# Two pairs of k-tiles of w_down: from direct column jobs behind the last run to the middle group of seven-product pairs

## The chip, the cores and the metric

The kernel runs on one core of a Trainium2 chip. The metric is the device time of one execution in microseconds (us); the figure given is the median of several runs. TensorE does the matmuls, VectorE (DVE), ScalarE (ACT) and GpSimd (POOL) the elementwise work, and the queues of SyncE (SP), ScalarE and POOL issue DMAs to 16 shared DMA engines.

## The reference

One encoder layer over 512 tokens of width 2048: a mixture of dilated window attention and gated linear attention, then a SwiGLU block, then a final RMSNorm. What matters here is the last step of the block and what follows it:

```python
h = rmsnorm(x, ffn_norm_w[l])
x = x + (jax.nn.silu(h @ w_gate[l]) * (h @ w_up[l])) @ w_down[l]   # (512 x 5632) @ (5632 x 2048)
return rmsnorm(x, final_norm_w)
```

All is float32. The kernel splits every operand of a large matmul into a high part (rounded to fp32r) and a low part (the rest), and sums three products: high by high, high by low, low by high.

## The kernel before, in words

The order of the instructions on every engine is written out by hand. TensorE, VectorE and ScalarE each work through their own instructions in program order; tiles come from pools of numbered slots, and a tile in a reused slot waits for the last users of the tile before it.

**Slots.** `s2` has 62 slots of 512 columns, `s4` 20 slots of 1024 columns, `ps` (in this phase "pu" in the profile) 8 PSUM banks. A slot is put back in program order and handed out oldest first (in `s4` a slot of the same kind first). One `s2` slot is held from the block's norm to the end (`rb[2]`).

**The product with w_down.** Its 5632 rows are 44 k-tiles of 128, taken as 22 pairs; its 2048 columns are four column blocks `c` of 512. The intermediate activations lie in DRAM (`gd`, one entry a pair). Before, the pairs are done in four ways, in this order:

- pairs 0 and 1: four direct column jobs (`job("B", ...)` with `evac_down`), 48 matmuls of 512 columns each, whose results are accumulated into `xd` in DRAM;
- pairs 2 to 17: class `Down`, seven-product pairs. A pair by a column block is a 2 x 2 block product with seven block products instead of eight. `Down.products` issues for each of the seven two token halves of three matmuls, 42 matmuls of 256 columns (lines 1625 to 1627);
- pairs 18 and 19: four more direct column jobs behind the runs (`evac_later`, `before_later`), lines 303 to 305, 48 matmuls of 512 columns each, whose results go straight to the residual;
- pairs 20 and 21 (`LAST = 40`): the tail (`finish`). It goes by token tiles `t` of 128, four column blocks each, 12 matmuls of 512 columns a block (lines 1815 to 1817); each block is added to the residual (`residual`, line 1449), squared on ScalarE (`squares`, line 409), and when a token tile is done its final norm is applied and it is sent out, so that only the last tile's end is uncovered.

**The runs of `Down`.** The pairs are in three groups X (2 to 7), Y (8 to 12) and Z (13 to 17), and there are ten runs, each a column block over some pairs:

```python
self.runs = [(0, X), (1, X), (2, X), (3, X + Y), (2, Y), (1, Y), (0, Y + Z), (1, Z), (2, Z), (3, Z)]
self.drop = {q: r for r, part in ((3, X), (6, Y), (9, Z)) for q in part}
```

A run holds seven banks. Runs 0 to 5 end with `evac`: each bank is copied to an `s2` slot and sent (or accumulated) to `md` in DRAM. A run from 6 on is `summed`: its seven partial results are fetched from `md` into seven `s2` slots (`fetch`, five pairs before the end of the run before) and copied into banks (`preload`, line 1598) while the last pair of the run before is multiplied; at its end `combine` (lines 1658 to 1675) makes the output of the column block, in seven steps that each put back a bank, and the generator `residuals` (line 1689), which is left on `urgent`, adds it to the residual tiles `x1[c]`.

**What a step needs.** The weights of a pair and column block are loaded by SP (line 1141), three sums are made on VectorE (`sums`, lines 1157 to 1159), and raw and sums are split: ScalarE casts the high part (line 1169), VectorE subtracts (line 1174). Where `by_dma` says so, the raw part's low part is made by an accumulating DMA of POOL instead (`part`, lines 1515 to 1517), and VectorE subtracts for the sums alone (line 1528).

**The activations' operands.** The generator `operands` makes a pair's: it loads `gd`, makes four differences (lines 1556 to 1559), and splits four sources (lines 1568 to 1572). It yields three times a pair; `make(n)` resumes it n times. A pair's operands hold 7 `s2` slots, from their making to the run named in `drop`. A pair is begun only if `len(s2.free) >= 9 + self.reserve`; the reserve is 4, and 11 in runs 4 and 5. If the pair of the step is not there yet, the loop makes it with no reserve. `make` is called behind the step's sums and splits and ahead of its matmuls.

**The stream of direct weights.** `st` loads the pieces of the direct jobs and of the tail (line 186; 512 KB each, two k-tiles) as long as fewer than `limit` are held, and `st.split(upto)` splits them half by half (line 201 on ScalarE, line 202 on VectorE). The direct jobs split three halves ahead, the later jobs a growing number ahead, so that all 16 halves of the tail are split under the later jobs. `g_load(j)` and `g_split(j)` load and split the activations of pair `j` for direct use (lines 1418, 1426 to 1430).

Of the kernel before, what the change touches and what calls it, by code (L numbers as in the profile page):

```python
# [120 lines left out]
def layer(nc, tc, x, attn_norm_w, w_in, rel_table, gw_f, gb_f, gw_b, gb_b, gla_norm_w, w_out,  # L121
# [7 lines left out]
    with tc.manual_schedule(), \  # L129
# [6 lines left out]
        s2 = Slots(p2, N2, 512, "a")  # L136
# [136 lines left out]
        def run_job(j):  # L273
# [6 lines left out]
            for i in range(j.n):  # L280
                if j.before:
                    j.before(i)
                st.load()
                st.split(j.first + i + AHEAD + (4 * j.tail + i if hasattr(j, "tail") else 0))
                _, _, wh, wl = st.halves[j.first + i]
# [1195 lines left out]
        class Down(Blocks):  # L1481
# [3 lines left out]
            def __init__(self, X, Y, Z):  # L1485
                self.runs = [(0, X), (1, X), (2, X), (3, X + Y), (2, Y), (1, Y), (0, Y + Z), (1, Z), (2, Z), (3, Z)]
                self.pairs = X + Y + Z
                self.drop = {q: r for r, part in ((3, X), (6, Y), (9, Z)) for q in part}
                self.begin([(r, q) for r, (c, part) in enumerate(self.runs) for q in part], 1, 256)
                self.x, self.parts, self.m, self.pre, self.seen = {}, {}, {}, [], set()  # L1490
                self.reserve = self.most = 4
                self.making = self.operands()

# [7 lines left out]
            def by_dma(self, i):  # L1501
                if i >= self.n:
                    return False
                r, q = self.seq[i]
                n = self.runs[r][1].index(q)
                return r == 3 or r == 6 and n > 5 or r > 6 and n in (0, 1, 4)

# [25 lines left out]
            def operands(self):  # L1533
# [14 lines left out]
                while raws or qs:  # L1548
                    load()
                    if not raws or len(s2.free) < 9 + self.reserve:  # L1550
                        yield
                        continue
# [142 lines left out]
            def run(self):  # L1695
                for i, (r, q) in enumerate(self.seq):
# [6 lines left out]
                    if left != 0:  # L1703
# [9 lines left out]
                        elif r != 3 and not self.by_dma(i + 2) and len(s4.free) > 4:  # L1713
                            self.sums(i + 3)
                            self.split(i + 2)
                    self.reserve = 11 if r in (4, 5) else 4
                    while q not in self.x:
                        self.reserve = 0
                        self.make(1)
                    self.make((r in (3, 6)) + i % 2)  # L1720
                    if n == max(len(part) - 5, 0) and r + 1 < len(self.runs) and self.summed(r + 1):
# [10 lines left out]
                    if r == len(self.runs) - 1:  # L1732
                        if n == 0:
                            g_load(LAST // 2 - 2)
                        if n == 2:
                            g_split(LAST // 2 - 2)
                            g_load(LAST // 2 - 1)
                            st.until, st.limit = None, 2
                            st.load()
                        if n == 3:  # L1740
                            st.split(later_first + 3)
                st.limit, st.big = 3, tail_first

        def evac_later(c):
            def f(banks):
                for t in range(4):
                    residual(c, t, banks[t])
            return f

        def before_later(c):  # L1750
            def f(i):
                j = LAST // 2 - 2 + (c + 1)
                if c and i == 0:
                    g_load(j)
                if i == (2 if c else 0) and c < 3:
                    g_split(j)
                run_urgent()
            return f

# [9 lines left out]
        down_pieces = len(st.pieces)  # L1769
        n_down = len(jobs)  # L1770
        later_first = len(st.halves)
        for c in range(4):
            j = job("B", [piece512(w_down, c * 512, k) for k in (LAST - 4, LAST - 2)], list(range(LAST - 4, LAST)),
                    lambda k: gT[k], evac_later(c), before=before_later(c), rate=1.0)
            j.tail = c
            if c == 3:
                j.drop = drop_g
        tail_first = len(st.halves)
        dn = Down(list(range(2, 8)), list(range(8, 13)), list(range(13, 18)))

# [10 lines left out]
        def finish():  # L1791

            first = len(st.halves)
            for c in range(4):
                st.add([piece512(w_down, c * 512, k) for k in range(LAST, 44, 2)])
            per = 44 - LAST

            def later(t, ys):
# [9 lines left out]
            def products(t, c, b, cols):  # L1808
                tok = slice(t * P, (t + 1) * P)
                o = b.t[:, cols]  # L1810
                for k in range(per):
                    st.split(first + c * per + k + 1)
                    _, _, wh, wl = st.halves[first + c * per + k]
# [57 lines left out]
        for n, j in enumerate(jobs):  # L1871
            if n == n_down:
                dn.run()
                start_tail()
            run_job(j)
            if n == n_out:
# [10 lines left out]
                ps = Slots(pcm.__enter__(), 8, 512, "pu")  # L1887
        drain()
        run_last()
# [28 lines left out]
```

## Time and profile before

| | us |
|---|---|
| median of three runs (lowest, highest) | 2190.3 (2189.37, 2192.0) |
| the profiled execution | 2190.92 |
| its span, first to last instruction | 2189.1 |

| phase of w_down in the profiled execution | start, us |
|---|---|
| direct jobs of pairs 0 and 1 | 1724.4 |
| runs 0 to 9 of `Down` | 1767.9 |
| direct jobs of pairs 18 and 19 | 2093.1 |
| tail | 2136.7 |
| last matmul starts | 2180.2 |

How to read it: the page gives for each engine its busy time and share of the span; a group of instructions by line has its count, busy time, mean duration and the idle time ahead of it with what ended that. In a list by order of time a row is start, length, engine, line, operation, output and inputs, count, and in square brackets the idle time of the engine ahead of it with its releaser. PE is TensorE's matmul and PEld its weight load. The listed duration of a matmul is longer than the distance between two of them, since they overlap; prices are taken from distances.

### The profile page before, as it was taken

The page shows a single profiled execution, that of the slowest core. Times are in us where ns is not written, and L with a number is a line of the kernel's source. Part 1 is how long each engine was busy: PE and PEld are TensorE (multiplying, and loading weights), DVE is VectorE, ACT ScalarE, POOL GpSimd, SP SyncE. Part 2 cuts the span into 40 slices and gives each one's busy share as a digit, 9 for nine tenths or more (in the row PEclk, how much of TensorE's full clock was granted, in tenths as well). Part 3 has the DMA queues.
Part 4 walks back from the last instruction along what each step waited for, and adds up shares of the span by engine and source line. Part 5 has one row for each costly group of instructions (what it writes and reads, how often), then busy time and mean ns, then how long its engine had stood idle before and what let it go on. Part 6 is the DMA issues. An engine that isn't in the chain of part 4 may idle for free.

```text
span 2189.1 us, 33329 instructions
## 1 busy us (share of the span) xinstructions
PE 2175.3 (99%) x12450; PEld 1908.5 (87%) x12450; DVE 1576.8 (72%) x2741; ACT 1217.8 (56%) x2032; POOL 325.4 (15%) x359
## 2 busy tenths in 40 slices
PE   9999999999999999999999999999999999999998
PEld 7888888888888888888888888888888899999987
DVE  4366665756456546888888888888888896888885
ACT  5344444444456436666666666666666665656642
POOL 0000000000000011222222222222222211121200
PEclk9999999999999999999999999999999999999999
DMA  6525635232222633889889898898888975888862
GB/s 210 161 84 142 162 90 144 91 97 87 97 87 88 211 106 103 195 193 210 203 195 211 192 211 202 196 211 193 208 204 198 288 183 172 240 212 230 254 220 77
DMA packets 255890, 375.19 MB, mean 171 GB/s; under 512 B 17999, under 2 KB 179455, under 8 KB 255728
## 3 DMA queue, kind: packets, MB, share of 16 engines
q1 hardware_dynamic: 188768, 252.03, 36.5%
q0 software_dynamic: 65776, 119.98, 28.1%
q8 instruction: 98, 1.61, 0.3%
q10 hardware_dynamic: 1184, 1.06, 0.2%
q14 instruction: 64, 0.52, 0.1%
HBM read 246.58 MB, written 35.19 MB: 129 GB/s over the span
## 4 chain that ended last, share of the span: by engine, by line
PE 94%; DVE 3%; DMA 2%; ACT 1%; issue 1%; SPq 0%; DVEq 0%; ACTq 0%
PE pd L1302 22%; PE pd L1308 11%; PE ps L303 5%; PE ps L304 5%; PE ps L305 5%; PE ps L295 5%; PE ps L296 5%; PE ps L297 5%; PE pe L1302 4%; PE pu L1626 4%; PE pu L1627 4%; PE pu L1625 4%; PE pe L1308 2%; DMA b<-in_w_down_dram 1%; PE pu L304 1%; PE pu L305 1%
## 5 line engine op out<-in xcount | busy, mean ns | idle before, releaser
L1302 PE MATMUL pd<-a,b 128*128 128x512 f32 x2112 | 528.4, 392 | 0.8 <-DVE a L1063 0.8
L1302 PEld LDWEIGHTS pd<-a,b 128*128 128x128 f32 x2112 | 378.9, 188 | 67.0 <-DVE a L1063 1.2
L1308 PEld LDWEIGHTS pd<-a,b 128*128 128x128 f32 x2112 | 288.5, 190 | 21.5
L1308 PE MATMUL pd<-a,b 128*128 128x256 f32 x2112 | 294.9, 282 | 0.0
L202 DVE TENSOR_TENSOR a<-b,a 128x512 fp32r<-128x512 f32 x288 | 193.1, 686 | 136.0 <-ACT a L201 124.1
L1209 POOL DMA_DIRECT2D b<-b x176 | 209.7, 1248 | 521.0 <-ACT b L1208 394.0
L1247 ACT CAST b<-b 128x1024 fp32r<-128x1024 f32 x176 | 185.3, 1053 | 166.3 <-DVE b L1233 138.4
L1626 PE MATMUL pu<-b,a 128*128 128x256 f32 x896 | 253.9, 283 | 0.9 <-DVE b L1174 0.9
L1625 PE MATMUL pu<-b,a 128*128 128x256 f32 x896 | 253.7, 283 | 0.5 <-ACT pu L1598 0.5
L1627 PE MATMUL pu<-b,a 128*128 128x256 f32 x896 | 253.5, 283 | 0.0
L1248 DVE TENSOR_TENSOR b<-b,b 128x1024 fp32r<-128x1024 f32 x176 | 214.9, 1221 | 50.3 <-ACT b L1247 26.4
L201 ACT CAST a<-b 128x512 fp32r<-128x512 f32 x288 | 170.2, 617 | 50.3 <-PE ps L305 22.3
L1626 PEld LDWEIGHTS pu<-b,a 128*128 128x128 f32 x896 | 172.0, 192 | 1.4 <-DVE b L1174 1.3
L1625 PEld LDWEIGHTS pu<-b,a 128*128 128x128 f32 x896 | 172.0, 192 | 0.9 <-ACT pu L1598 0.9
L1627 PEld LDWEIGHTS pu<-b,a 128*128 128x128 f32 x896 | 172.0, 192 | 0.0
L1330 DVE TENSOR_TENSOR a<-pd,a 128x512 f32<-128x512 f32 x132 | 91.4, 692 | 95.7 <-ACT a L1329 95.7
L1208 ACT ACTIVATE b<-b 128x768 fp32r<-128x768 f32 x176 | 149.1, 847 | 4.7 <-PE ps L305 2.9
L1210 ACT CAST b<-b 128x768 fp32r<-128x768 f32 x176 | 145.2, 825 | 0.6 <-PE ps L305 0.6
L1329 ACT COPY a<-pd 128x512 f32<-128x512 f32 x132 | 77.5, 587 | 102.0 <-PE pd L1308 102.0
L1230 DVE TENSOR_TENSOR b<-b 128x512 f32<-128x512 f32 x176 | 120.4, 684 | 0.0
L595 ACT CAST b<-ps 128x512 fp32r<-128x512 f32 x64 | 37.6, 587 | 142.9 <-PE ps L529 142.9
L295 PE MATMUL ps<-a,a 128*128 128x512 f32 x288 | 115.3, 400 | 0.0
(278 smaller groups left out, 4506.4 us busy)
## 6 DMA issues: line engine op xcount, KB each, us to landing
b<-b POOLq DMA_DIRECT2D x200, 384.0 KB, 5.5
b<-in_w_gate_dram SPq DMA_DIRECT2D x88, 512.0 KB, 3.8
b<-in_w_up_dram SPq DMA_DIRECT2D x88, 512.0 KB, 4.4
b<-in_w_down_dram SPq DMA_DIRECT2D x88, 512.0 KB, 6.3
b<-in_w_in_dram SPq DMA_DIRECT2D x48, 512.0 KB, 4.5
b<-in_w_in_dram SPq DMA_DIRECT2D x94, 256.0 KB, 4.2
b<-in_w_out_dram SPq DMA_DIRECT2D x32, 512.0 KB, 5.3
a<-a SPq DMA_DIRECT2D x96, 128.0 KB, 2.4
```

The source lines that it names most:

```text
L201: act.copy(h[2].t, r)
L202: dve.tensor_tensor(h[3].t, r, h[2].f, op=OP.subtract)
L295: mm(o, wh.t[:, c], xh.t, start=first, stop=False)
L1208: act.activation(lo.t, r, AF.Copy, scale=-1.0)
L1209: pool.dma_start(out=lo.f, in_=r, accum_op=OP.add)
L1247: act.copy(hi.t, self.S[i].t)
L1248: dve.tensor_tensor(lo.t, self.S[i].t, hi.f, op=OP.subtract)
L1302: mm(o, wh.t[:, p, k], x_.t.rearrange("p s t -> p (s t)"), start=first and p == 0, stop=False, skip_group_check=True)
L1308: mm(o[:, 256:512], wl.t[:, p, k], x_.t[:, 0], start=False, stop=last and p == 1, skip_group_check=True)
L1625: mm(o, xh[:, t], wh, start=first and not loaded and h == 0, stop=False, skip_group_check=True)
L1626: mm(o, xh[:, t], wl, start=False, stop=False, skip_group_check=True)
L1627: mm(o, xl[:, t], wh, start=False, stop=last, skip_group_check=True)
```

## The change

The four direct jobs of pairs 18 and 19 are gone, with `evac_later` and `before_later`. Y becomes pairs 8 to 14 (seven) and Z pairs 15 to 19 (five). The low part by DMA in run 6 moves from the steps behind the sixth pair to those behind the eighth. The rule for beginning a pair's operands takes the reserve only for pairs later than the step's own (`need`); in run 3 from the eighth pair on the reserve is 11 and one more `make` is issued on every other step. In the last run the activations of pairs 20 and 21 are loaded on its first two steps and split on its second and third; the third loads up to four pieces of the tail's weights, and behind the fourth pair twelve halves are split at once, into `s4` slots as long as more than three are free. The last four halves are split in the tail, two each in its second and third column block of the first token tile, where the rest of `urgent` runs too, one resumption a column block.

```diff
-                st.split(j.first + i + AHEAD + (4 * j.tail + i if hasattr(j, "tail") else 0))
+                st.split(j.first + i + AHEAD)
...
+                self.need = self.pairs[0]
...
-                return r == 3 or r == 6 and n > 5 or r > 6 and n in (0, 1, 4)
+                return r == 3 or r == 6 and n > 7 or r > 6 and n in (0, 1, 4)
...
-                    if not raws or len(s2.free) < 9 + self.reserve:
+                    if not raws or len(s2.free) < 9 + (raws[0][0] > self.need) * self.reserve:
...
-                    self.reserve = 11 if r in (4, 5) else 4
+                    self.reserve = 11 if r in (4, 5) or r == 3 and n > 6 else 4
+                    self.need = q
                     while q not in self.x:
-                        self.reserve = 0
                         self.make(1)
-                    self.make((r in (3, 6)) + i % 2)
+                    self.make((r in (3, 6)) + (i % 2 or r == 3 and n > 6))
...
                     if r == len(self.runs) - 1:
-                        if n == 0:
-                            g_load(LAST // 2 - 2)
+                        if n < 2:
+                            g_load(LAST // 2 + n)
+                        if n == 1:
+                            g_split(LAST // 2)
                         if n == 2:
-                            g_split(LAST // 2 - 2)
-                            g_load(LAST // 2 - 1)
-                            st.until, st.limit = None, 2
+                            g_split(LAST // 2 + 1)
+                            st.until, st.limit, st.big = None, 4, tail_first
                             st.load()
                         if n == 3:
-                            st.split(later_first + 3)
-                st.limit, st.big = 3, tail_first
...
-        for c in range(4):
-            j = job("B", [piece512(w_down, c * 512, k) for k in (LAST - 4, LAST - 2)], list(range(LAST - 4, LAST)),
-                    lambda k: gT[k], evac_later(c), before=before_later(c), rate=1.0)
-            j.tail = c
-            if c == 3:
-                j.drop = drop_g
+                            st.split(tail_first + 12)
...
-        dn = Down(list(range(2, 8)), list(range(8, 13)), list(range(13, 18)))
+        dn = Down(list(range(2, 8)), list(range(8, 15)), list(range(15, 20)))
...
+            upto = [first + 12]
...
-                    st.split(first + c * per + k + 1)
+                    if t == 0 and c and k % 2 == 0:
+                        upto[0] += 1
+                        st.split(upto[0])
...
                         products(t, c, b, whole)
+                        if t == 0 and c < 3:
+                            run_urgent()
                         residual(c, t, b)
...
         for n, j in enumerate(jobs):
-            if n == n_down:
-                dn.run()
-                start_tail()
             run_job(j)
...
-        drain()
+        dn.run()
+        start_tail()
         run_last()
```

More of the change, by code (lines that the diff above doesn't have):

```diff
@@ L1732, in run @@
                     if r == len(self.runs) - 1:
-                        if n == 0:
-                            g_load(LAST // 2 - 2)
+                        if n < 2:
+                            g_load(LAST // 2 + n)
+                        if n == 1:
+                            g_split(LAST // 2)
                         if n == 2:
-                            g_split(LAST // 2 - 2)
-                            g_load(LAST // 2 - 1)
-                            st.until, st.limit = None, 2
+                            g_split(LAST // 2 + 1)
+                            st.until, st.limit, st.big = None, 4, tail_first
                             st.load()
                         if n == 3:
-                            st.split(later_first + 3)
-                st.limit, st.big = 3, tail_first
[L1744 to L1758, printed above, removed]
+                            st.split(tail_first + 12)
         LAST = 40
@@ L1769, in layer @@
         down_pieces = len(st.pieces)
-        n_down = len(jobs)
-        later_first = len(st.halves)
-        for c in range(4):
-            j = job("B", [piece512(w_down, c * 512, k) for k in (LAST - 4, LAST - 2)], list(range(LAST - 4, LAST)),
-                    lambda k: gT[k], evac_later(c), before=before_later(c), rate=1.0)
-            j.tail = c
-            if c == 3:
-                j.drop = drop_g
         tail_first = len(st.halves)
-        dn = Down(list(range(2, 8)), list(range(8, 13)), list(range(13, 18)))
+        dn = Down(list(range(2, 8)), list(range(8, 15)), list(range(15, 20)))
         wf = []
```

## The prediction

> **What bounds the kernel now.** I read four views: the page (busy shares and chain), the table by stretches of time, the rows of the matmul lines, and then the order of time of VectorE, ScalarE and the queues where the edit acts.
>
> ```profile
> PE 2175.3 (99%) x12450; PEld 1908.5 (87%) x12450; DVE 1576.8 (72%) x2741; ACT 1217.8 (56%) x2032; POOL 325.4 (15%) x359
> PE 94%; DVE 3%; DMA 2%; ACT 1%; issue 1%; SPq 0%; DVEq 0%; ACTq 0%
> L1625 PE MATMUL pu<-b,a x896: 277/283/384, 1767.9 to 2092.7; 128*128 128x256 f32 x180
> L1815 PE MATMUL pu<-b,a x68: 278/389/389, 2136.7 to 2180.0; 128*128 128x512 f32 x60, 128*128 128x256 f32 x8
> 1858.40:1913.70 55.30, 55.30 (x463) 55.30 (x462) 47.72 (x84) 36.93 (x57) 10.95 (x16) 1.00 0.88 238
> 1964.00:2014.30 50.30, 50.30 (x422) 50.30 (x421) 43.28 (x76) 32.64 (x48) 12.30 (x16) 1.00 0.95 242
> 2014.30:2041.00 26.70, 25.26 (x205) 24.49 (x204) 23.88 (x36) 16.99 (x24) 4.80 (x7) 1.00 0.68 189
> 2067.90:2093.10 25.20, 25.20 (x212) 25.20 (x212) 20.01 (x30) 12.63 (x18) 5.19 (x9) 1.00 0.88 307
> 2093.10:2136.70 43.60, 43.60 (x194) 35.91 (x194) 37.38 (x60) 19.81 (x36) 0.00 (x0) 1.00 0.44 163
> ```
>
> In the stretch rows the columns are length, then busy time of TensorE, weight load, VectorE, ScalarE, POOL, the clock, the DMA share and GB/s. TensorE is the bound: 99% busy, 94% of the chain, clock 1.00. In w_down it loses time only in 2014 to 2041: 1.4 us idle, and its 205 matmuls at the pace of run 3 (below) would need 24.5 of the 26.70, so some 2.2 us. So matmul time moves the end one to one, and everything else counts only where it keeps TensorE waiting. But VectorE is close behind: 47.72 of 55.30 us in run 3, 43.28 of 50.30 in run 6.
>
> **The matmuls.** A pair in a run is 42 matmuls of 256 columns. Run 3 is 11 pairs, 462 matmuls in 55.3 us: 0.1197 us each, 5.03 us a pair. The direct jobs behind the runs are 192 matmuls of 512 columns from 2093.1 to 2136.7: 0.227 each. Removed: 43.6 us. Added: 2 pairs x 4 column blocks x 42 = 336 x 0.1197 = 40.2 us. **Term 1: -3.4 us**, though an eighth of the columns goes: the narrow matmul costs more than half of the wide one.
>
> The Trainium skill, "TensorE: Matmul & The Clock Gate", section "Back-to-back issue gap", gives about 131 ns for a 512-column and 81 ns for a 128-column matmul in a sustained stream with weight loads. By it the removed matmuls would be 25 us and the added ones, at an estimate between its two figures (98 ns), 33 us: the edit would lose 8 us. The trace's 227 ns disagrees, so this takes no chance below.
>
> **VectorE's own work** grows:
>
> ```profile
> L202 DVE TENSOR_TENSOR a<-b,a 128x512 fp32r<-128x512 f32 x32 | 20.9, 682 | 6.5 <-ACT a L201 6.5
> L1157 DVE TENSOR_TENSOR b<-b 128x512 f32<-128x512 f32 x64 | 44.1, 689 | 4.4 <-PE pu L1626 1.8 <-DMA b<-in_w_down_dram 1.3
> L1159 DVE TENSOR_TENSOR b<-b,b 128x256 f32<-128x256 f32 x64 | 27.2, 425 | 2.2
> L1174 DVE TENSOR_TENSOR b<-b,b 128x1024 fp32r<-128x1024 f32 x40 | 48.9, 1221 | 0.0
> L1174 DVE TENSOR_TENSOR b<-b,b 128x768 fp32r<-128x768 f32 x40 | 38.2, 954 | 18.8 <-ACT b L1169 15.0 <-ACT b L1515 3.6
> ```
>
> Per column block a direct pair costs it two splits, 1.4 us; a pair in a run 0.69 + 2 x 0.43 + 1.22 + 0.95 = 3.7 (2.8 where the last is left to a transfer). Such work lies beside TensorE unless it is late; three places follow where it is.
>
> **Run 3: pair 14's operands.** The pool of 512-column slots has 62; one is held by `rb[2]`, a pair's operands hold 7. With six pairs held, 62 - 1 - 42 = 19 are free, and the reserve of 11 asks for 9 + 11 = 20. The trace of before shows this refusal:
>
> ```profile
> 1895.68 0.42 DVE L1556 TENSOR_TENSOR a<-b 128x256 f32<-128x256 f32 x1
> 1905.75 0.42 DVE L1556 TENSOR_TENSOR a<-b 128x256 f32<-128x256 f32 x1
> 1907.22 0.42 DVE L1569 SCALAR_TENSOR_TENSOR a<-b,a 128x256 fp32r<-128x256 f32 x1
> 1907.55 0.69 DVE L1572 TENSOR_TENSOR a<-b,a 128x512 fp32r<-128x512 f32 x1
> 1909.68 2.09 DVE L1174 TENSOR_TENSOR b<-b,b 128x768 fp32r<-128x768 f32 x2
> 1911.68 1.28 DVE L1572 TENSOR_TENSOR a<-a,a 128x512 fp32r<-128x512 f32 x2
> 1969.76 0.42 DVE L1556 TENSOR_TENSOR a<-b 128x256 f32<-128x256 f32 x1
> ```
>
> The sixth held pair starts at 1905.75; the next only at 1969.76, in run 6: runs 4 and 5, with the reserve of 11, make none. After the edit the same reserve holds in run 3 from its eighth pair on. Pairs 8 to 13 are made by its tenth step; pair 14 is refused until the step that multiplies it (the thirteenth), where the loop makes it with no reserve. So its operands are issued in the very step that needs them. When does VectorE get there? In before's last step of run 3 TensorE starts at 1858.4 + 50.3 = 1908.7, and the next set's subtractions (L1174), which stand ahead of the making, end at 1911.77, 3.1 us later. From L1556 to the end of L1569 (1905.75 to 1907.64) are 1.9 us more until B11's low half, which the third matmul reads (0.24 us into the step): 3.1 + 1.9 - 0.24 = 4.7 us. The low halves of T2, the third product, follow by 6.9 us, just after TensorE would come to them. **Term 2: +4.7 us.** Lower end 0 (VectorE gets ahead while making is refused), upper 7.
>
> **Runs 5 and 6.** Seven Y pairs hold 49 slots: 12 are free, and the fetch of seven partial results for run 6 leaves 5. Run 5's last step copies out seven banks, so the seventh copy reuses the first one's slot and must wait for its transfer:
>
> ```profile
> 1962.77 3.53 POOL L1649 DMA_DIRECT2D md<-a  x4 [19.51 <-ACT a L1646]
> md<-a POOLq DMA_DIRECT2D x42, 256.0 KB, 5.8
> 1964.45 1.88 DVE L1644 COPY a<-pu 128x512 f32<-128x512 f32 x3
> 1987.18 2.09 DVE L1174 TENSOR_TENSOR b<-b,b 128x768 fp32r<-128x768 f32 x2
> ```
>
> Issued at 1962.77 and 5.8 us to landing make 1968.6, where the last copy now starts about 1965.7: VectorE is 2.9 us late into run 6. What waits for it are the sets of weights queued behind. Before has no lead left there: run 6's sixth pair starts at 1964.0 + 25.2 = 1989.2, and its subtractions end at 1989.27. In run 6 steps 7 and 8 also become VectorE's own. **Term 3: +2.5 us**, between -2.2 (run 7's loss goes, the longer runs giving a lead) and +5 (steps 7 and 8, at 3.7 us and 1.9 of making, each 0.6 over TensorE's 5.03, on top of a full 2.9 and what run 7 adds).
>
> **The last run and the tail.** Run 9 starts at 2067.95; its fifth pair runs from 2088.1 to 2093.1. Two g splits, now on its second and third step, put one extra (1.2 us) ahead of the fourth pair's subtractions: about 0.3 us of waiting. Then:
>
> ```profile
> 2084.58 1.22 DVE L1528 TENSOR_TENSOR b<-b,b 128x1024 fp32r<-128x1024 f32 x1
> 2078.11 9.63 SPq L186 DMA_DIRECT2D b<-in_w_down_dram  x7
> 2086.00:2088.00 2.00, 2.00 (x19) 2.00 (x19) 0.00 (x0) 0.00 (x0) 0.00 (x0) 1.00 1.03 410
> 2088.50 1.14 ACT L201 CAST a<-b 128x512 fp32r<-128x512 f32 x2 [4.25 <-DMA b<-in_w_down_dram]
> 2090.78 0.62 ACT L201 CAST a<-b 128x512 fp32r<-128x512 f32 x1 [1.14 <-DMA b<-in_w_down_dram]
> 2092.04 0.68 DVE L1658 TENSOR_TENSOR b<-pu,a 128x512 f32<-128x512 f32 x1
> 2096.23 0.68 DVE L1659 TENSOR_TENSOR b<-a,pu 128x512 f32<-128x512 f32 x1
> 2094.74 5.30 ACT L201 CAST a<-b 128x512 fp32r<-128x512 f32 x10
> 2100.68 3.69 DVE L202 TENSOR_TENSOR a<-b,a 128x512 fp32r<-128x512 f32 x6
> 2098.03 2.07 DVE L1689 SCALAR_TENSOR_TENSOR a<-b,small,a 128x512 f32<-128x512 f32 x3
> 2139.61 0.75 DVE L1449 SCALAR_TENSOR_TENSOR a<-pu,small,a 128x512 f32<-128x512 f32 x1 [1.97 <-PE pu L1817]
> 2140.39 0.63 ACT L409 ACTIVATE a<-a 128x512 f32<-128x512 f32 x1 [18.43 <-DVE a L1449]
> 2140.93 0.19 ACT L409 ACTIVATION_READ_ACCUMULATOR a<-a 128x1 f32 x1
> ```
>
> Before puts three splits behind the fourth pair; the first waits until 2088.50 for its piece and the third until 2090.78, because the DMA engines are full (share 1.03 at 410 GB/s). Twelve stand there now. At 410 GB/s a 512 KB piece is 1.3 us, so pieces 3 to 6 land by about 2096.1; with 0.53 us a cast and 0.605 a subtraction the twelfth is done at 2097.9. Only behind them, on both engines, come the copies and sums that empty the last pair's banks. The tail's second column block lacks a bank from 2096 to 2097.9. Then in VectorE's order: seven combining steps (2092.04 to 2096.9 in before, 4.8 us): 2102.7; two residuals 1.3 and the tail's own 0.7: 2104.7; ScalarE's square and its read, 0.7, ahead of the cast of half 13: 2105.4; cast and subtraction: 2106.6, half 14: 2107.2; two residuals and the tail's second: 2109.2; its square, cast, subtraction: half 15 at 2111.1, half 16 at 2111.7. TensorE wants these four halves in the tail's fourth column block, which without a wait would start at 2093.1 + 3 x 2.73 = 2101.3; it ends at 2112.2 instead of 2104.0. **Term 4: +8.2 us**, the 0.3 and the bank's wait within it. Lower end: VectorE's share of the chain without any hand-over, 18.6 us from the last set's end (L1528, 2085.8), still ends at 2104.4 against 2103.3, +1; upper 10. I take the worked chain, as its first half is measured in place.
>
> The other three token tiles, the final residuals and the output are unchanged; the moved SP issues (two gd loads, eight pieces) stand where before issued sixteen pieces and four gd loads, and POOL's four loads of the final weights stay behind the last run: nothing beyond the landing times taken, whose cover is that stretch's free SP. The removed jobs' splits, residuals and g splits ran under their own matmuls: 0.
>
> **Sum.** -3.4 + 4.7 + 2.5 + 8.2 = +12.0, on the profiled execution's 2190.9: 2202.9. That execution lies 0.6 above the median 2190.3, so 2202.3.
>
> **The rivals.**
> One late place only: VectorE, unoccupied while making is refused, reaches pair 14 in time, or pieces land early enough for the burst. For it: a pair's making is 3.8 us of VectorE (the rows from 1905.75 on: 1.9 + 0.6 + 1.3), and in steps 11 and 12 none of it is left. Against it: L1174 there starts only when TensorE frees slots. Then -3.4 + 8.2 = 2195.7, or -3.4 + 4.7 + 2.5 = 2194.7.
> It is faster: VectorE's lead covers all of it. That needs 4.7 us of lead at pair 14, and in the tail the twelfth split done 8 us earlier, by 2090. Then 2190.9 - 3.4 = 2187.5, and with run 7's 2.2 gone 2185.3, faster only there. Against it: the fifth pair's last subtraction itself ends at 2085.8 in before.
> Worse: run 6's deficit grows into run 7, which already stalls, and pieces land later behind the seven fetches: upper ends, -3.4 + 7 + 5 + 10 = 2209.5.
>
> **How the numbers follow.** A run to run difference of 0.2% (4.4 us) is about what can be told from none: faster is below 2185.9, slower above 2194.7. All three late places (2198 to 2207): 0.50. One only (2192 to 2198): 0.25, of which 0.15 slower. None: 0.15, of which 0.07 faster. Worse: 0.10. Together slower 0.75, same 0.18, faster 0.07. The range 2187 to 2209 leaves out about 0.07 below and 0.08 above; for the likeliest case alone 2198 to 2207.
>
> **What would show it.** Right: VectorE's L1572 as the releaser of a TensorE wait of 4 to 5 us in run 3's last step; the ScalarE and VectorE split lines (L201, L202) ahead of the combining steps, and as releasers of the tail's fourth column block, 5 us or more; matmul counts 3024 and 192 fewer. Wrong: no TensorE idle over 1 us between 1900 and 2115, or pair 14's operands made a step before its use.

## The result, and the profile after

The change made the kernel slower by 0.7%: 2207.0 us (median of 6; 2201.85 to 2207.85) against 2190.6 (2188.25 to 2192.23), ratio 1.0072, 95% interval 1.0059 to 1.0085. The profiled execution took 2207.85, its span 2206.1, 17.0 over before's. The prediction was 2202.3, range 2187 to 2209.

From the page of the changed kernel: the busy shares, the chain and two of the three matmul lines of the runs. Line numbers are those of the file that ran; in the changed one 1626 to 1628 were 1625 to 1627, 1557 to 1573 were 1556 to 1572, 1528 and 1529 were 1527 and 1528, 1516 was 1515, 1645 was 1644, 1665 was 1664, and the tail's 1795 to 1797 were 1815 to 1817.

```profile
PE 2180.1 (99%) x12594; PEld 1918.7 (87%) x12594; DVE 1589.5 (72%) x2759; ACT 1227.2 (56%) x2038; POOL 327.2 (15%) x361
PE 95%; DVE 2%; DMA 1%; ACT 1%; issue 0%; SPq 0%; DVEq 0%; ACTq 0%
L1628 PE MATMUL pu<-b,a 128*128 128x256 f32 x1008 | 287.4, 285 | 4.7 <-DVE a L1570 4.7
L1626 PE MATMUL pu<-b,a 128*128 128x256 f32 x1008 | 287.4, 285 | 2.4 <-ACT a L1569 2.4
```

The shares hardly tell anything: TensorE is 99% busy in both. The idle column does: 4.7 us on L1570 and 2.4 on L1569, the splits of a pair's operands. Taken in order of time, these are all rows of the changed kernel's TensorE behind 1900 that carry an idle time:

```profile
1920.45 0.39 PE L1626 MATMUL pu<-b,a 128*128 128x256 f32 x1 [1.47 <-ACT a L1569]
1923.19 0.42 PE L1628 MATMUL pu<-b,a 128*128 128x256 f32 x1 [2.24 <-DVE a L1570]
2056.63 0.39 PE L1626 MATMUL pu<-b,a 128*128 128x256 f32 x1 [0.89 <-ACT a L1569]
2059.56 0.39 PE L1628 MATMUL pu<-b,a 128*128 128x256 f32 x1 [2.42 <-DVE a L1570]
2132.09 0.39 PE L1627 MATMUL pu<-b,a 128*128 128x256 f32 x1 [0.34 <-DVE b L1174]
2146.73 0.50 PE L1795 MATMUL pu<-b,a 128*128 128x512 f32 x1 [1.68 <-ACT a L1665]
2155.21 0.56 PE L1795 MATMUL pu<-b,a 128*128 128x512 f32 x1 [2.73 <-ACT b L201]
2155.94 0.79 PE L1796 MATMUL pu<-b,a 128*128 128x512 f32 x1 [0.16 <-DVE b L202]
2159.79 0.80 PE L1795 MATMUL pu<-b,a 128*128 128x512 f32 x1 [1.35 <-ACT b L201]
```

Three places: the last pair of run 3, the last pair of run 6, the tail's first token tile. From the starts of the matmuls (every 42nd is a new pair) the length of each stage follows:

| stage | before, us | after, us | at the pace of 0.12 us a matmul | lost after |
|---|---|---|---|---|
| run 3 (11, then 13 pairs) | 55.4 | 71.2 | 65.5 | 5.7 |
| runs 4 and 5 | 50.4 | 70.6 | 70.6 | 0 |
| run 6 (10, then 12 pairs) | 50.4 | 65.8 | 60.5 | 5.3 |
| run 7 | 27.6 | 25.2 | 25.2 | 0 (before 2.4) |
| run 9 | 25.2 | 25.8 | 25.2 | 0.6 |
| direct jobs behind the runs | 43.7 | none | | |
| tail, to its last matmul's start | 43.6 | 54.8 | | 11.2 |

Matmuls -3.4, waits 5.7 + 5.3 + 0.6 + 11.2, less run 7's 2.4: +17.0, the span's difference. But the idle times in the rows above sum to 13.3 us, and the losses to 22.8. Part of the rest is in the clock; the changed kernel by stretches (columns as in the prediction):

```profile
1920.00:1924.00 4.00, 1.31 (x6) 1.10 (x7) 3.97 (x9) 2.14 (x5) 0.00 (x0) 0.93 0.64 188
1924.00:1928.00 4.00, 4.00 (x25) 4.00 (x24) 2.40 (x5) 2.13 (x4) 1.41 (x3) 0.65 0.47 184
1928.00:1932.00 4.00, 4.00 (x36) 4.00 (x35) 0.87 (x1) 3.60 (x7) 2.43 (x5) 1.00 0.71 287
2060.00:2064.00 4.00, 4.00 (x23) 4.00 (x22) 2.69 (x5) 1.96 (x4) 0.00 (x0) 0.58 1.03 361
2150.00:2154.00 4.00, 2.48 (x11) 1.71 (x10) 3.86 (x6) 0.07 (x1) 0.00 (x0) 1.00 0.00 0
2154.00:2158.00 4.00, 2.62 (x6) 1.68 (x6) 2.81 (x5) 1.68 (x4) 0.00 (x0) 0.69 0.00 0
2158.00:2162.00 4.00, 2.65 (x7) 1.50 (x6) 2.43 (x4) 1.99 (x5) 0.00 (x0) 0.50 0.00 0
2162.00:2166.00 4.00, 4.00 (x11) 3.16 (x10) 1.53 (x6) 1.61 (x6) 0.00 (x0) 0.53 0.02 4
2166.00:2170.00 4.00, 4.00 (x19) 3.28 (x18) 3.68 (x7) 0.35 (x1) 0.00 (x0) 1.00 0.55 202
```

A stretch of 4 us at full clock shows 36 matmuls of 256 columns; behind the waits it shows 25 and 23, with the granted clock at 0.65 and 0.58. In the tail it falls to 0.50, and 11 matmuls of 512 columns go where 19 go later. TensorE counts as busy there, so no idle column shows it. The mean clock is 0.994 against before's 0.998.

### The profile page after: what moved, and what is told of

The parts are those of the page before. It is cut to its first block, busy times and chain, and to the rows that moved or that the text cites. A ratio compares the mean times of both kernels' runs of the same rounds, so it can differ in the third digit from the quotient of the medians.

```text
span 2206.1 us, 33648 instructions
## 1 busy us (share of the span) xinstructions
PE 2180.1 (99%) x12594; PEld 1918.7 (87%) x12594; DVE 1589.5 (72%) x2759; ACT 1227.2 (56%) x2038; POOL 327.2 (15%) x361
## 4 chain that ended last, share of the span: by engine, by line
PE 95%; DVE 2%; DMA 1%; ACT 1%; issue 0%; SPq 0%; DVEq 0%; ACTq 0%
PE pd L1302 22%; PE pd L1308 11%; PE ps L303 5%; PE ps L304 5%; PE ps L305 5%; PE ps L295 5%; PE ps L296 5%; PE ps L297 5%; PE pu L1628 5%; PE pu L1627 5%; PE pu L1626 5%; PE pe L1302 4%; PE pe L1308 2%; PE ps L529 1%; DMA b<-in_w_down_dram 1%; PE ps L537 1%
## 5 line engine op out<-in xcount | busy, mean ns | idle before, releaser
L1628 PE MATMUL pu<-b,a 128*128 128x256 f32 x1008 | 287.4, 285 | 4.7 <-DVE a L1570 4.7
L1626 PE MATMUL pu<-b,a 128*128 128x256 f32 x1008 | 287.4, 285 | 2.4 <-ACT a L1569 2.4
L1627 PE MATMUL pu<-b,a 128*128 128x256 f32 x1008 | 287.3, 285 | 0.3 <-DVE b L1174 0.3
L202 DVE TENSOR_TENSOR a<-b,a 128x512 fp32r<-128x512 f32 x274 | 184.5, 686 | 133.2 <-ACT a L201 122.1
L1628 PEld LDWEIGHTS pu<-b,a 128*128 128x128 f32 x1008 | 195.2, 194 | 5.1 <-DVE a L1570 5.1
L1626 PEld LDWEIGHTS pu<-b,a 128*128 128x128 f32 x1008 | 195.2, 194 | 2.8 <-ACT a L1569 2.8
L1627 PEld LDWEIGHTS pu<-b,a 128*128 128x128 f32 x1008 | 195.3, 194 | 0.6 <-DVE b L1174 0.5
L201 ACT CAST a<-b 128x512 fp32r<-128x512 f32 x274 | 162.7, 617 | 46.3 <-PE ps L305 22.3
L1210 ACT CAST b<-b 128x768 fp32r<-128x768 f32 x176 | 145.3, 825 | 0.6 <-PE ps L305 0.6
L1169 ACT CAST b<-b 128x768 fp32r<-128x768 f32 x92 | 82.3, 942 | 89.3 <-issue 71.7
L1174 DVE TENSOR_TENSOR b<-b,b 128x768 fp32r<-128x768 f32 x92 | 98.0, 1088 | 30.3 <-ACT b L1169 26.6
```

Of the source, the lines that this page charges most:

```text
L201: act.copy(h[2].t, r)
L202: dve.tensor_tensor(h[3].t, r, h[2].f, op=OP.subtract)
L1210: act.copy(hi.t, r)
L1626: mm(o, xh[:, t], wh, start=first and not loaded and h == 0, stop=False, skip_group_check=True)
L1627: mm(o, xh[:, t], wl, start=False, stop=False, skip_group_check=True)
L1628: mm(o, xl[:, t], wh, start=False, stop=last, skip_group_check=True)
```

## The experiments

My theory: three local orders, not a lack of VectorE time, keep TensorE waiting, and a lower clock behind the waits adds to the loss. The rival: VectorE is full, and the waits only show where it is late.

**1. Pair 14 may be begun earlier.**

```diff
-                    self.reserve = 11 if r in (4, 5) or r == 3 and n > 6 else 4
+                    self.reserve = 11 if r in (4, 5) else 10 if r == 3 and n > 6 else 4
```

> The changed kernel with one number altered: in run 3 from the eighth pair on the reserve is 10 instead of 11, so that with 19 slots free pair 14 may be begun. Theory A (its operands are refused until the step that multiplies them): they are begun two steps earlier, the two TensorE waits in run 3's last step (1.5 and 2.2 us) go, and with them the lower clock behind them; run 3 goes from 71.2 us to 65.5 (13 x 5.04), the whole by 5 to 6 us to about 2201. Rival B (VectorE is full in run 3, the refusal only shows where it is late): the wait goes elsewhere in runs 3 and 4, and the whole moves by less than 2 us.

Run 3 took 65.5 us, no wait left in it, none in runs 4 and 5; the whole 2197.9, ratio to before 1.0039 (1.0026 to 1.0052). So the refusal at 19 free slots was the cause. The gain, some 9 us, is more than run 3 explains: in the profiled execution run 6 was 64.7 and the tail 52.7 us too, though the edit touches neither. Such differences show again below: where nothing in them was edited, run 6 took 62.5 to 67.0 us and the tail 52.3 to 55.3, one profile a kernel. In the tail it is the clock, as experiment 7 shows; what moves run 6's waits was not settled.

**2. Pair 19 made earlier.**

```diff
-                    self.make((r in (3, 6)) + (i % 2 or r == 3 and n > 6))
+                    self.make((r in (3, 6)) + (i % 2 or r == 3 and n > 6 or r == 6))
```

> The changed kernel with one more resumption of the operand generator on every other step of run 6, so that pair 19 is made a step or more earlier. Theory A (pair 19's splits stand in VectorE's order behind the first set of run 7, which waits for a w_down load): the waits of 0.9 and 2.4 us at the start of run 6's last step go, run 6 from 65.8 to about 60.5, the whole by 5 to 5.5 us to about 2201.5. Rival B (run 6 has more VectorE work than TensorE time, as the prediction had it: 3.7 + 1.9 us a step against 5.03): earlier making only brings the wait forward, run 6 stays above 63 us, the whole within 2.5 us of 2207.

2204.3, ratio 1.0065 (1.0048 to 1.0082); run 6 still 64.7 us. The two waits of its last pair are gone, but theory A missed: a wait came forward, to the weights of run 6's eighth pair. TensorE, then VectorE of this kernel in order of time:

```profile
2038.18 0.39 PE L1627 MATMUL pu<-b,a 128*128 128x256 f32 x1 [2.52 <-DVE b L1174]
2032.98 1.29 DVE L1573 TENSOR_TENSOR a<-a,a 128x512 fp32r<-128x512 f32 x2 [1.42 <-ACT a L1572]
2034.19 0.42 DVE L1557 TENSOR_TENSOR a<-b 128x256 f32<-128x256 f32 x1
2037.18 2.09 DVE L1174 TENSOR_TENSOR b<-b,b 128x768 fp32r<-128x768 f32 x2
```

The making (L1573, L1557) now stands ahead of the set (L1174) that TensorE needs first.

**3. Another order around the last run's end.**

```diff
-                            st.split(tail_first + 12)
+                            st.split(tail_first + 8)
...
-                    if t == 0 and c and k % 2 == 0:
-                        upto[0] += 1
-                        st.split(upto[0])
...
-                        if t == 0 and c < 3:
+                        if t == 0 and c < 2:
+                            st.split(first + 12 + 4 * c)
+                        if t == 0 and c > 1:
                             run_urgent()
```

> The changed kernel with another order around the last run's end, all instructions kept: eight halves are split behind the fourth pair instead of twelve; the next four stand behind the tail's first column block's matmuls and ahead of its residual, the last four behind the second's; the two resumptions of the residual generator come in the third and fourth column block. Theory A (the tail waits because of the order on VectorE and ScalarE: splits ahead of the bank's emptying, residuals and squares ahead of the last splits): the bank's wait of 1.8 us goes to under 0.5, the wait for halves 13 to 16 to under 2 us, the first token tile from 23.2 us (2142.1 to 2165.4) to 11 to 14, the whole by 8 to 11 us to 2196 to 2199. Rival B (the pieces land too late, the DMA engines being full): with the same loads the fourth column block still waits 4 us or more, the whole moves by under 4 us.

2196.4, ratio 1.0032 (1.0021 to 1.0043); the tail 47.7 us instead of 54.8, the bank's wait gone. Same instructions, same loads: the order was the cause of 7 of the 11 us, the clock's share included, as this tail stayed at full clock. (Most of the rest of what the whole gained is run 6, 62.5 us here without an edit to it.) Waits of 2.1 us on the ninth to twelfth halves and of 0.9 on the thirteenth remained.

**4. The three edits together.**

> The changed kernel with the three edits together: reserve 10 in run 3, one more resumption in run 6, the other order at the last run's end. Theory A (three separate late places on top of a gain of 3.3 us in the matmuls and 2.5 us in run 7, whose stall the changed kernel does not have): the gains add up, 5.7 + 5.4 + 9 of the 16.8 us lost and gained back, so about 2187 (2185 to 2190), 1.5 to 5 us under before's 2190.6. Rival B (VectorE is at its limit, what is mended in one place is late in the next): 2193 or more, with new waits in runs 7 to 9.

2191.3, ratio 1.0008 (0.9998 to 1.0017): 15.7 of the 16.4 us came back, but it is neither theory's number. Run 3 was 65.5, run 6 still 63.1, the tail 47.5.

**5 and 6. What is it in run 6?** In the changed kernel, ScalarE, then VectorE:

```profile
2053.75 0.84 ACT L1516 ACTIVATE b<-b 128x768 fp32r<-128x768 f32 x1 [2.63 <-DMA b<-in_w_down_dram]
2055.22 1.04 ACT L1528 CAST b<-b 128x1024 fp32r<-128x1024 f32 x1
2048.55 0.42 DVE L1557 TENSOR_TENSOR a<-b 128x256 f32<-128x256 f32 x1
2056.29 1.23 DVE L1529 TENSOR_TENSOR b<-b,b 128x1024 fp32r<-128x1024 f32 x1 [3.53 <-ACT b L1528]
2059.08 0.42 DVE L1570 SCALAR_TENSOR_TENSOR a<-b,a 128x256 fp32r<-128x256 f32 x1
```

Pair 19's differences are made at 2048.55, its splits only at 2059.08. Between them VectorE stands idle 3.53 us at L1529, the first set of run 7. The cast of that set (L1528) stands on ScalarE behind the part of the second set that is left to a transfer (`part(i + 3)`, L1516), and it is the second set's load, not the first's, that ScalarE waits for. VectorE is not full there; it is held up. The two readings were put apart on the mended run 3 and tail order: one kernel relieves VectorE, the other changes the order.

```diff
-                return r == 3 or r == 6 and n > 7 or r > 6 and n in (0, 1, 4)
+                return r == 3 or r == 6 and n > 5 or r > 6 and n in (0, 1, 4)
```

> The changed kernel with reserve 10 in run 3, the other order at the last run's end (as before: eight halves, then four, then four), and in run 6 the low part made by a transfer from the seventh pair on instead of the ninth, so that VectorE subtracts 0.95 us less in each of two more steps; the operand generator as in the changed kernel. Theory B (run 6 is short of VectorE time, which is why making earlier only brought the wait forward to its eighth pair's weights): run 6 goes to under 61.5 us (60.5 is the pace), the whole to about 2188 to 2190. Theory A (pair 19's last two splits stand behind the first set of run 7, which waits for its load): that queue is unchanged, run 6 keeps a wait on L1570 at the start of its last step and stays at 62.5 to 65.8 us; the whole 2191 to 2195.

```diff
                         if left == 1:
+                            if r == 6:
+                                self.make(2)
                             self.split(i + 2)
```

> The changed kernel with reserve 10 in run 3, the other order at the last run's end, and one edit in run 6: in its last but one step two resumptions of the operand generator come ahead of the split of run 7's first set instead of behind it; the number of steps made from the ninth pair on by a transfer is the changed kernel's. Theory A (pair 19's splits are late only because they stand behind that set): the wait on L1570 goes, run 6 is 60.5 to 61.5 us, the whole 2188 to 2190. Theory B (VectorE time): a wait of 1 us or more stays in run 6 or comes at run 7's first pair, whose set is now later; run 6 and 7 together over 87.5 us (60.5 + 25.2 is 85.7), the whole 2191 or more.

With less work for VectorE run 6 was 64.2 us and the wait of 2.0 us on L1570 stayed (2192.8, ratio 1.0013, 1.0004 to 1.0023). With the other order run 6 was 60.5 us, no wait in it, run 7 26.1 (2189.9, ratio 1.0003, 0.9993 to 1.0012). TensorE in the first of the two kernels, then VectorE in the second, where the last pair starts at 2048.8:

```profile
2051.01 0.39 PE L1628 MATMUL pu<-b,a 128*128 128x256 f32 x1 [1.99 <-DVE a L1570]
2046.78 0.43 DVE L1570 SCALAR_TENSOR_TENSOR a<-b,a 128x256 fp32r<-128x256 f32 x1 [0.80 <-ACT a L1569]
```

So the wait on L1570 is the queue, as theory A had it. But part of what it cost turns up in run 7, which loses 0.9 us here and 1.8 to 2.1 in experiments 10 to 12 with the same order, waiting for its weights' subtractions. Runs 6 and 7 together take 87.5 to 88.8 us there, not below the 87.5 that theory B named, against 87.7 to 92.2 with the changed kernel's order. That VectorE has room around run 7 is not shown.

**7 and 8. Keeping the clock up.** Matmuls of no use fill the waits; VectorE and ScalarE are as late as before.

```diff
+                    if r == 3 and n == len(part) - 1:
+                        spin(28)
                     self.products(i)
...
+                        if t == 0 and c == 3:
+                            spin(22)
                         b = ps.get()
```

> The changed kernel with matmuls of no use put into two of its waits, their results not read: 28 of 128 columns on a zero tile ahead of the last pair of run 3 (some 3.4 us at full clock) and 22 ahead of the fourth column block of the tail's first token tile (2.6 us). Nothing else is altered, so VectorE and ScalarE are as late as before. Theory A (what the prediction missed, some 5 us, is the lower granted clock behind each wait: 17 matmuls at 0.215 us after run 3's, some 20 at 0.425 us in the tail): run 3 goes from 71.2 to 69.5 us, the tail from 54.8 to about 51.5, the whole by 4 to 5 us to 2202 to 2203, the mean clock from 0.994 to 0.997. Rival B (the matmuls behind a wait are slow because their operands still trickle in): the lengths stay within 0.7 us, or grow by the added matmuls.

The tail took 51.6 us instead of 54.8, with the clock at 1.00 throughout:

```profile
2150.00:2154.00 4.00, 4.00 (x38) 4.00 (x37) 2.71 (x5) 1.75 (x4) 0.00 (x0) 1.00 0.00 0
2154.00:2158.00 4.00, 2.80 (x13) 1.83 (x12) 2.71 (x6) 1.75 (x4) 0.00 (x0) 1.00 0.00 0
2158.00:2162.00 4.00, 4.00 (x19) 3.26 (x19) 2.31 (x9) 1.85 (x6) 0.00 (x0) 1.00 0.01 4
```

So 3.1 us of the tail's loss are the clock. The tails without a filler agree: with half clock for 10.24 us they took 54.8 and 55.3 (the changed kernel and experiment 2), with half clock for 3.41 us 52.7 and 52.3 (experiments 1 and 8). In run 3 the filler was twice as long as I had reckoned (each matmul of no use appears as two, 28 took 6.2 us), longer than the wait; run 3 was 71.8 us, which shows nothing. The whole was 2204.9, ratio 1.0068 (1.0053 to 1.0083). So again, with 16 in run 3 alone:

> The changed kernel with 16 matmuls of no use (each takes two of about 0.11 us, 3.5 us together) ahead of the last pair of run 3, and nothing else. With 28 of them the filler was 6.2 us, longer than the wait it filled, so run 3's length told nothing, though the clock stayed at 1.00. Theory A (of run 3's 5.9 us over its pace, some 1.8 are the lower clock behind the wait): with the filler shorter than the wait, the clock stays at 1.00 and run 3 goes from 71.2 to 69.3 to 69.8 us; the whole by 1.5 to 2 us to about 2205. Rival B (the matmuls there are slow because operands arrive late): 71 us or more.

Run 3 took 70.1 us, 1.1 less, with the clock at 1.00 in each stretch from 1916 to 1928 (0.93 and 0.65 above), the operands as late as ever; 2205.0 for the whole, ratio 1.0067 (1.0053 to 1.0081). The gain in run 3 is below the 1.4 to 1.9 expected, and on the clock's side; the whole of neither kernel can be told from the changed kernel's.

**9. Pieces earlier.** On the mended run 3, with eight halves split behind the tail's first column block:

```diff
                             g_load(LAST // 2 + n)
+                        if n == 0:
+                            st.until, st.limit = None, 2
+                            st.load()
...
+                        if t == 0 and c == 0:
+                            st.split(first + 16)
```

> The changed kernel with reserve 10 in run 3 and another end of the last run: the first two pieces of the tail's weights are loaded on its first step instead of its third, when the DMA engines have room; eight halves are split behind the fourth pair, and the other eight behind the first column block's matmuls, ahead of all residuals of the tail; run 6 as in the changed kernel. Theory A (with the order mended, what is left of the tail's wait, 3.9 us, is VectorE standing idle for pieces, 1.3 and 2.4 us): VectorE's idle time ahead of its first eight subtractions goes under 1 us, the tail from 47.5 us to 43.6 to 44.5, the whole to 2189 to 2191 with run 6's wait left in. Rival B (VectorE's work itself doesn't fit between the last set and the fourth column block): the tail stays at 46 us or more, the whole 2192 or more.

2192.7, ratio 1.0013 (1.0003 to 1.0022). The tail was 43.6 us, without a wait. But the last run was 29.9: the two pieces waited in SP's queue for a slot, and the second activation load behind them landed so late that ScalarE stood at it:

```profile
2131.16 0.63 ACT L1426 ACTIVATE a<-b 128x512 fp32r<-128x512 f32 x1 [10.01 <-DMA b<-gd]
```

The wait had moved, not gone.

**10 to 12. Versions meant to beat both.** The tenth puts both activation loads first and adds the sixth's order; the eleventh also splits the activations a step later.

> Reserve 10 in run 3, the operand generator ahead of run 7's first set in run 6's last but one step, eight halves split behind the fourth pair and eight behind the tail's first column block, and both activation loads on the last run's first step, ahead of the first two pieces of weights, which are loaded on its second (with the pieces ahead of the second activation load, that load came 4 us late and held up the last run). Theory A (order alone made the changed kernel slower): run 3 65.5, run 6 60.5, runs 7 to 9 77.2, tail 43.6 to 44.5; the whole 2186 to 2187, ratio to before 0.998 to 0.9987. Rival B (VectorE's work between run 9's last set and the fourth column block doesn't fit): the last run or the tail keeps 2.5 us or more, the whole within 0.1% of before.

> The same, with the two splits of the activations one step later in the last run (third and fourth step, where before had its one), so that none stands ahead of the fourth pair's subtractions. Theory A: the last run's wait of 0.5 us goes (25.8 to 25.2) and nothing comes in its place, as the tail needs them only 5 us later: 0.6 us less than the kernel beside it. Rival B: the later activation split pushes the first eight halves back by 1.2 us, and the tail gains a wait of about that size.

Both 2190.4, ratio 1.0000 (0.9992 to 1.0009, and 0.9991 to 1.0009). Run 3 was 65.5 and run 6 60.9 and 61.5, but run 7 was back at 27.3, close to the 27.6 before the change, and the tail kept 3.7 and 3.0 us: rival B of the tenth by the numbers. In the eleventh the last run's small wait went (25.2), and the tail's longest grew from 1.8 to 2.5, about half of what its rival B said. TensorE in run 7 of the tenth, then from the eleventh SP's wait and VectorE:

```profile
2070.36 0.39 PE L1627 MATMUL pu<-b,a 128*128 128x256 f32 x1 [0.88 <-DVE b L1174]
SPq L1418 <- DVE b L1174: 7.3, 1, 7.3
2131.26 1.29 DVE L202 TENSOR_TENSOR b<-b,b 128x512 fp32r<-128x512 f32 x2 [2.99 <-ACT b L201]
```

The second activation load waits 7.3 us for a large slot, and all pieces queue behind it on SP. Many 512-column slots are free then, so the last kernel loads those activations there (and takes the fifth's transfers in run 6):

```diff
+                if j >= LAST // 2:
+                    graw[j] = [s2.get(), s2.get()]
+                    for f in (1, 0):
+                        sp.dma_start(out=graw[j][f].t, in_=gd[j][:, f * 512:(f + 1) * 512])
+                    return
                 graw[j] = s4.get(F32, [P, 2, 512])
```

> The mended kernel once more (reserve 10, the operand generator ahead of run 7's first set, splits of the activations a step later, eight halves behind the fourth pair and eight behind the tail's first column block), with two edits. First, the activations of pairs 20 and 21 are loaded into free 512-column slots instead of 1024-column ones, so that neither they nor the first two pieces of weights, now on the last run's first step, queue for a large slot (the kernel beside it had SP wait 7.3 us for one, and VectorE 3.0 us for the second piece). Second, run 6 leaves the low part to a transfer from the seventh pair on. Theory A (what is left of the tail's wait is the queue for slots in front of the loads): VectorE's idle time ahead of its first eight subtractions is under 1 us, last run and tail together 68.8 to 69.8 us (71.8 before this edit), and with run 6 and 7 at 85.7 to 88 the whole is 2186 to 2188, ratio to before 0.998 to 0.999. Rival B (VectorE's work itself): the tail keeps a wait of 2 us or more though the pieces are there; within 0.1% of before.

2186.8 us (median of 11) against before's 2190.2 beside it, ratio 0.9984 (0.9975 to 0.9993): faster by 3.4 us, a small gain, but one that its interval keeps apart from none. Run 6 60.5, run 7 27.0, last run 25.2, tail 44.5 us; beside the eleventh, runs 6 and 7 are 1.3 us shorter and the tail 2.1, and which edit gave what was not taken apart. Six halves are now split in one go; VectorE still waits 2.1 us for the fourth piece, more than the 1 us expected, but it costs TensorE only 0.56 (L1803 is the tail's matmul):

```profile
2125.65 3.69 DVE L202 TENSOR_TENSOR b<-b,b 128x512 fp32r<-128x512 f32 x6
2131.44 1.29 DVE L202 TENSOR_TENSOR b<-b,b 128x512 fp32r<-128x512 f32 x2 [2.11 <-ACT b L201]
2138.17 0.50 PE L1803 MATMUL pu<-b,a 128*128 128x512 f32 x1 [0.56 <-DVE b L202]
```

## Why the prediction was right, and where its steps were not

The whole came at 2207.0, the upper edge of the likeliest case (2198 to 2207).

**The matmuls, -3.4.** Right. 13 pairs without a wait take 65.5 us in every kernel with run 3 mended, 0.12 us a matmul, and the last kernel, where little is lost but in run 7 (1.8 us, 2.4 before) and the tail (0.9), keeps 3.4 us. The rule that I had set aside (the Trainium skill, "TensorE: Matmul & The Clock Gate", section "Back-to-back issue gap": 131 ns sustained for 512 columns) does not agree with the result: by it the matmuls would have lost 8 us, and the stages show 3.4 gained.

**Run 3, +4.7.** Place and cause were right, and the time without the clock; 5.7 measured. VectorE in the changed kernel:

```profile
1921.26 0.42 DVE L1557 TENSOR_TENSOR a<-b 128x256 f32<-128x256 f32 x1
1922.72 0.42 DVE L1570 SCALAR_TENSOR_TENSOR a<-b,a 128x256 fp32r<-128x256 f32 x1
```

TensorE should have started the step at 1918.8; the making starts 2.5 us later and B11's low half is there at 1923.14, 4.3 us behind the start. The idle times make 3.7 us; of the other 2.0, experiment 8 shows 1.1 to be the clock, which the sum did not have. The sign that I had named was the wrong line: the waits, 1.47 and 2.24 us instead of one of 4 to 5, were released by L1569 and L1570 (1568 and 1569 before), not by what was L1572.

**Runs 5 and 6, +2.5.** The sum is near (5.3 lost in run 6, 2.4 gained in run 7: +2.9), but that is luck: the reason was wrong. The seventh copy of run 5 does wait for its slot, 2.30 us as against my 2.9:

```profile
2003.68 0.69 DVE L1645 COPY a<-pu 128x512 f32<-128x512 f32 x1 [2.30 <-DMA md<-a]
```

But it reached no matmul: TensorE does not wait in run 6 before its last pair. What I took as a deficit of VectorE over steps 7 and 8 was not felt, and the step that failed is "What waits for it are the sets of weights queued behind". In its place stands pair 19, made in the step before its use, behind a set that is held up by a load (experiments 2, 5 and 6). The gain in run 7 hangs on that wait too: with run 6's order mended, run 7 lost 0.9 to 2.1 us again. I had worked out for pair 14 in which step the operands are issued and not for pair 19.

**The tail, +8.2.** 11.8 measured, with run 9's 0.6. Step by step it held. The bank came at 4.6 us into the tail (worked out 4.8); half 13's high part let the fourth column block start at 13.1 us (12.9); half 15's cast ended at about 17.6 (17.4). The idle times there are 2.73, 0.16 and 1.35 us, 4.2 where I had named 5 or more. Of the 3.6 us over the term 3.1 are the clock again, shown by the filler. That the order and not the loads is most of it is experiment 3; that the loads have a share is 9 and 12.

So one thing explains most of the 4.9 us between 12.0 and 16.9 (the profiled executions): no term had the clock, which costs 3.1 us in the tail and 1.1 in run 3. It fell for 3.4 us in run 6 too, where no experiment took it apart.

## What to carry to other kernels

When an edit removes slack work, ask for each generator or queue in which program step its last consumer's input is issued, and what stands ahead of it there; a refused slot (19 of 20) or a load that holds up a set turns up as a wait some steps on. A tile that must be ready right after a burst belongs ahead of work that only has to be done sometime, on each in-order engine and on the queue that issues its load. Behind a TensorE wait of some 2 us look at the clock column: the wait may cost more than the idle time says.

## What the runs showed of the hardware that I had not expected

The granted clock fell after waits well under 4 us, but not after all of them. Run 3's two waits, 1.47 and 2.24 us with two matmuls between them, were followed by 3.4 us (1923.4 to 1926.8) at 0.215 us a 256-column matmul instead of 0.12, the tail's 2.73 us by half clock until 2165.8. A single wait of 1.68 us (2146.73) left it at 1.00, and so did one of 2.79 us in the tail of experiment 5 (2142.37), longer than the 2.73.

So the length of a wait does not decide it. In each of the fourteen traces every change of the clock lies on a grid of 3.41 us, and a fall goes with how little TensorE was busy in one such stretch. Two stretches of the changed kernel, each with the one behind it, then the two that share experiment 5's wait:

```profile
1920.00:1923.41 3.41, 0.72 (x3) 0.51 (x4) 3.38 (x8) 2.10 (x5) 0.00 (x0) 1.00 0.56 148
1923.41:1926.83 3.42, 3.42 (x18) 3.42 (x18) 2.99 (x6) 1.22 (x3) 0.95 (x2) 0.50 0.58 226
2145.28:2148.69 3.41, 1.96 (x9) 1.62 (x10) 3.15 (x6) 3.17 (x5) 0.00 (x0) 1.00 0.13 50
2148.69:2152.11 3.42, 3.42 (x17) 2.82 (x15) 3.28 (x6) 0.00 (x0) 0.00 (x0) 1.00 0.00 0
2140.55:2143.96 3.41, 1.59 (x7) 1.34 (x8) 3.41 (x6) 0.00 (x0) 0.00 (x0) 1.00 0.00 0
2143.96:2147.37 3.41, 2.24 (x9) 1.32 (x8) 2.11 (x5) 2.55 (x6) 0.00 (x0) 1.00 0.00 0
```

Behind the first 30 us the traces hold 8829 stretches at full clock. Half clock followed 31 of them, and these are the 31 in which TensorE was least busy, for some 47% of the time at most (by the profile's modelled ends); of the other 8798 the lowest is the row with 1.59 us above, also some 47%. Full clock came back behind a stretch at half clock that was 94% busy or more, and not behind one of 81% or less; at 91% both occur. So two waits of one length can cost more or less by where they fall on the grid.

The Trainium skill, "TensorE: Matmul & The Clock Gate", section "What's actually happening", has the clock halved after an idle window of about 3.4 us that runs free of the kernel. The halving, the length and the grid agree with these traces; that a stretch with TensorE busy for up to 47% of it is enough goes beyond what it says.
